# A gated linear unit: one activation and one product per tile, with only the waits that others do not imply

## The chip, the cores and the metric

The kernel runs on one core of one Trainium2 chip. The metric is the device time of a run in microseconds (us). Most runs of a kernel here agree within 0.3%. Every kernel named below was built, profiled and compared with the reference on the chip. Each was timed in rounds beside the kernel before on the same chip.

## The reference

```python
x = np.random.randn(8192, 8192).astype(np.float32)

def reference(x):
    a, b = np.split(x, 2, axis=-1)
    return a * (1 / (1 + np.exp(-b)))
```

268.4 MB go in and 134.2 MB come out, and each output element needs one sigmoid and one product.

## The kernel before

A tile is 256 rows of x, two rows (R = 2) on each of 128 partitions: 8 MB in and 4 MB out, 32 tiles. There are two slots for inputs and two for outputs. Loads are issued by the sync engine (queue 1), stores by the scalar engine (queue 10).

```python
    pool = ctx.enter_context(tc.tile_pool(name="io", bufs=2))
    for i in range(n_tiles):
        x_sb = pool.tile([P, R * n_cols], fp32)
        o_sb = pool.tile([P, R * half], fp32)
        load = nc.sync.dma_start(out=x_sb, in_=x_t[i])
        n = 4 if i == n_tiles - 1 else 1      # the last tile in 8 pieces
        w = half // n
        for r in range(R):
            for c in range(n):
                # ... a, b: columns of x_sb; cols: columns of o_sb
                nc.scalar.activation(out=b, in_=b, func=SIG)
                nc.vector.tensor_mul(out=o_sb[:, cols], in0=a, in1=b)
                if n > 1:
                    nc.scalar.dma_start(out=out_t[i, :, cols], in_=o_sb[:, cols])
        if n == 1:
            nc.scalar.dma_start(out=out_t[i], in_=o_sb)
```

The framework that builds the kernel works out the waits, and it also chooses the order of the instructions on each engine. Cut here: the lines that move the first load ahead of the program's start, which the change leaves alone.

Of the kernel before, what the change touches and what calls it, by code (L numbers as in the profile page):

```python
# [1 line left out]

# [4 lines left out]


def _tiles(ctx, tc, x, out):
    nc = tc.nc  # L10
    P = nc.NUM_PARTITIONS
    fp32 = mybir.dt.float32
    SIG = mybir.ActivationFunctionType.Sigmoid

    n_rows, n_cols = x.shape
    half = n_cols // 2
    R = 2
    n_tiles = n_rows // (P * R)
    x_t = x.rearrange("(n p r) m -> n p (r m)", p=P, r=R)
    out_t = out.rearrange("(n p r) m -> n p (r m)", p=P, r=R)  # L20

    pool = ctx.enter_context(tc.tile_pool(name="io", bufs=2))
    first = None

    for i in range(n_tiles):
        x_sb = pool.tile([P, R * n_cols], fp32)
        o_sb = pool.tile([P, R * half], fp32)
        load = nc.sync.dma_start(out=x_sb, in_=x_t[i])
        first = first or load
        n = 4 if i == n_tiles - 1 else 1  # L30
        w = half // n
        for r in range(R):
            for c in range(n):
                lo = r * n_cols + c * w
                a = x_sb[:, lo : lo + w]
                b = x_sb[:, lo + half : lo + half + w]
                cols = slice(r * half + c * w, r * half + (c + 1) * w)
                nc.scalar.activation(out=b, in_=b, func=SIG)  # L38
                nc.vector.tensor_mul(out=o_sb[:, cols], in0=a, in1=b)  # L39
                if n > 1:  # L40
                    nc.scalar.dma_start(out=out_t[i, :, cols], in_=o_sb[:, cols])  # L41
        if n == 1:
            nc.scalar.dma_start(out=out_t[i], in_=o_sb)
    return first


@with_exitstack
def kernel(
    ctx: ExitStack,
    tc: tile.TileContext,  # L50
    x: bass.AP,
    out: bass.AP,
):



    nc = tc.nc
    with ExitStack() as pools:
        _tiles(pools, tc, x, out)
    tc.close()  # L60
    tc.compile()  # L61
    blocks = nc.main_func.blocks
    entry, body = blocks[0].instructions, blocks[1].instructions
    SP = mybir.EngineType.SP
    at = next(k for k, i in enumerate(body) if i.engine == SP)
    load = body[at]
    assert load.opcode == "DMACopy" and not load.sync_info.on_wait
    del body[at]
    where = next(k for k, i in enumerate(entry) if i.engine == SP and i.opcode == "Drain")
    entry.insert(where, load)  # L70


# [1 line left out]
_INS = ['x']  # L74
_OUTS = [((8192, 4096), 'float32')]


# [23 lines left out]
```

## Time and profile before

| | before |
|---|---|
| time, median (lowest to highest) | 936.02 us (935.64 to 936.99, 6 runs) |
| span of the profiled run | 933.9 us |
| rate of all transfers | 431 GB/s |
| busy: vector engine, scalar engine | 280.9 us (30%), 230.0 us (25%) |
| load, issue to landing (median) | 45.5 us |
| store, issue to landing (median) | 41.7 us |

How to read it: the two engines that compute are idle for over two thirds of the time. "Issue to landing" runs from the moment an engine hands a transfer to its queue until the data have arrived. The prediction shows the lines of the profile that stand behind these numbers, and reads them.

### The profile page before, as it was taken

The numbers are of one execution on the slowest core, as the hardware profiler recorded it, in microseconds if no ns is written. First come the engines' busy times: TensorE is split into PE (matmuls) and PEld (weight loads), VectorE is DVE, ScalarE is ACT, GpSimd is POOL, SyncE is SP. The second block draws the span as 40 slices with busy tenths as digits, with TensorE's granted clock in tenths as the row PEclk, the third lists the DMA queues.
The fourth block names the chain that finished last, engine by engine and source line by source line (L and its number), as shares of the span: only waits on it lengthen the run. The fifth ranks groups of instructions, "written<-read, shape, count | busy, mean of one in ns | idle before, by whom it ended". The sixth has DMA issues, their size and how long they took to land.

```text
span 933.9 us, 410 instructions
## 1 busy us (share of the span) xinstructions
DVE 280.9 (30%) x70; ACT 230.0 (25%) x71; POOL 0.2 (0%) x4
## 2 busy tenths in 40 slices
DVE  0333321333213333133331333312333123331234
ACT  1313331133311333203332033320233202333023
POOL 0000000000000000000000000000000000000000
DMA  9999999999999999999999999999999999999998
GB/s 404 420 434 431 453 418 429 439 434 449 420 456 404 452 424 427 449 425 451 412 459 410 438 438 425 451 421 452 413 449 421 431 445 443 429 420 453 410 446 362
DMA packets 10226, 402.67 MB, mean 431 GB/s; under 512 B 1136, under 2 KB 1136, under 8 KB 2160
## 3 DMA queue, kind: packets, MB, share of 16 engines
q1 hardware_dynamic: 4608, 268.44, 66.5%
q10 hardware_dynamic: 5616, 134.22, 33.3%
q14 instruction: 2, 0.02, 0.0%
HBM read 268.44 MB, written 134.22 MB: 431 GB/s over the span
## 4 chain that ended last, share of the span: by engine, by line
DMA 78%; DVE 15%; ACT 6%; issue 0%; DVEq 0%; ACTq 0%
DMA x_sb<-in_x_dram 78%; DVE o_sb L39 15%; ACT x_sb L38 6%; DVEq L61 0%; ACTq L41 0%; ACTq L38 0%
## 5 line engine op out<-in xcount | busy, mean ns | idle before, releaser
L39 DVE TENSOR_TENSOR o_sb<-x_sb 128x4096 f32<-128x4096 f32 (+1 forms) x70 | 280.9, 4056 | 647.2 <-ACT x_sb L38 647.2
L38 ACT ACTIVATE x_sb<-x_sb 128x4096 f32<-128x4096 f32 (+1 forms) x70 | 228.7, 3315 | 695.9 <-DMA x_sb<-in_x_dram 691.8
L38 ACT ACT_TABLE_LOAD x1 | 1.3, 1283 | 0.8 <-PEq L85 0.8
L85 POOL MEMSET const-uint8-127<- 128x1 uint8 x1 | 0.1, 103 | 0.0
L85 POOL MEMSET const-bfloat16-1.0<- 128x1 bf16 x1 | 0.1, 102 | 0.0
L85 POOL MEMSET const-float32-0.0<- 128x1 f32 x1 | 0.1, 99 | 0.2 <-issue 0.2
L85 POOL MEMSET const-float32-1.0<- 128x1 f32 x1 | 0.1, 99 | 0.0
## 6 DMA issues: line engine op xcount, KB each, us to landing
out_dram<-o_sb ACTq DMA_DIRECT2D x31, 4096.0 KB, 41.7
out_dram<-o_sb ACTq DMA_DIRECT2D x8, 512.0 KB, 6.2
x_sb<-in_x_dram SPq DMA_DIRECT2D x32, 45.5
```

The source lines that it names most:

```text
L38: nc.scalar.activation(out=b, in_=b, func=SIG)
L39: nc.vector.tensor_mul(out=o_sb[:, cols], in0=a, in1=b)
L85: nc = _bacc.Bacc("TRN2", target_bir_lowering=False, num_devices=1)
```

## The change

Its intent: fewer and larger instructions in tiles 1 to 30 (a sigmoid of 8192 elements per partition instead of two of 4096, the product likewise), and no waits that follow from other waits. A wait for an output slot moves from the product to the sigmoid in odd tiles. Each sigmoid is pinned to the program's order on its engine. In the last tile the store of a piece follows the next piece's sigmoid.

```diff
-    pool = ctx.enter_context(tc.tile_pool(name="io", bufs=2))
+    pool = ctx.enter_context(tc.tile_pool(name="io", bufs=1))
+    xs = [pool.tile([P, R * n_cols], fp32, name=f"x_sb{k}") for k in range(SLOTS)]
+    os = [pool.tile([P, R * half], fp32, name=f"o_sb{k}") for k in range(SLOTS)]
+    def implied(later, *earlier):
+        for e in earlier:
+            tc.declare_no_dep(later.ins, e.ins, reason="follows from the waits that are kept")
...
+        load = nc.sync.dma_start(out=xs[i % SLOTS], in_=x_t[i])
+        implied(load, *old["loads"], *old["sigs"])
+        if i == 0:
+            parts = [(slice(r, r + 1), slice(0, half)) for r in range(R)]
+        elif i < n_tiles - 1:
+            parts = [(slice(0, R), slice(0, half))]
+        else:
+            # ... eight pieces of 1024 columns, as before
...
+        for k, (r, c) in enumerate(parts):
+            b = rows[:, r, 1, c]
+            sig = nc.scalar.activation(out=b, in_=b, func=SIG)
+            mul = nc.vector.tensor_mul(out=packed[:, r, c], in0=rows[:, r, 0, c], in1=b)
+            implied(sig, *old["sigs"], *old["muls"], *old["loads"])
+            implied(mul, *old["muls"], *old["loads"], *now["loads"])
+            by_sigmoid = i % 2 == 1 and len(parts) == 1
+            implied(mul, *(s for s in old["stores"] if by_sigmoid or s not in freed))
+            if by_sigmoid:
+                for s in freed:
+                    tc.add_manual_dep(sig.ins, s.ins.name, DEP, reason="frees the output slot")
+            tc.keep_in_program_order(sig)
...
+            if i == n_tiles - 1 and k > 0:
+                store(chunks[k - 1])
+        store(chunks[-1] if i == n_tiles - 1 else slice(0, R * half))
```

More of the change, by code (lines that the diff above doesn't have):

```diff
@@ L11, in _tiles @@
     P = nc.NUM_PARTITIONS
+    DEP = mybir.DependencyInfo(mybir.DependencyClass.Sync, mybir.DependencyReason.DATA)
     fp32 = mybir.dt.float32
@@ L17, in _tiles @@
     R = 2
+    SLOTS = 2
     n_tiles = n_rows // (P * R)
@@ L20, in _tiles @@
     out_t = out.rearrange("(n p r) m -> n p (r m)", p=P, r=R)
-    pool = ctx.enter_context(tc.tile_pool(name="io", bufs=2))
-    first = None
-    for i in range(n_tiles):
-        x_sb = pool.tile([P, R * n_cols], fp32)
-        o_sb = pool.tile([P, R * half], fp32)
-        load = nc.sync.dma_start(out=x_sb, in_=x_t[i])
-        first = first or load
-        n = 4 if i == n_tiles - 1 else 1
-        w = half // n
-        for r in range(R):
-            for c in range(n):
-                lo = r * n_cols + c * w
-                a = x_sb[:, lo : lo + w]
-                b = x_sb[:, lo + half : lo + half + w]
-                cols = slice(r * half + c * w, r * half + (c + 1) * w)
-                nc.scalar.activation(out=b, in_=b, func=SIG)
-                nc.vector.tensor_mul(out=o_sb[:, cols], in0=a, in1=b)
-                if n > 1:
-                    nc.scalar.dma_start(out=out_t[i, :, cols], in_=o_sb[:, cols])
-        if n == 1:
-            nc.scalar.dma_start(out=out_t[i], in_=o_sb)
@@ L44, in _tiles @@
-    return first
+    pool = ctx.enter_context(tc.tile_pool(name="io", bufs=1))
[4 more added lines that the diff above has]
+            tc.declare_no_dep(later.ins, e.ins, reason="follows from the waits that are kept")
+    gone = [{k: [] for k in ("loads", "sigs", "muls", "stores")} for _ in range(SLOTS)]
+    last_stores = [[] for _ in range(SLOTS)]
@@ new lines, in _tiles, with store @@
+    for i in range(n_tiles):
+        old = gone[i % SLOTS]
+        freed = last_stores[i % SLOTS]
+        now = {k: [] for k in old}
+        rows = xs[i % SLOTS].rearrange("p (r h m) -> p r h m", r=R, h=2)
+        packed = os[i % SLOTS].rearrange("p (r m) -> p r m", r=R)
+        load = nc.sync.dma_start(out=xs[i % SLOTS], in_=x_t[i])
+        implied(load, *old["loads"], *old["sigs"])
+        now["loads"].append(load)
+        if i == 0:
[3 more added lines that the diff above has]
+        else:
+            w = half // 4
+            parts = [
+                (slice(r, r + 1), slice(c * w, (c + 1) * w)) for r in range(R) for c in range(4)
+            ]
+        def store(cols):
+            ins = nc.scalar.dma_start(out=out_t[i, :, cols], in_=os[i % SLOTS][:, cols])
+            now["stores"].append(ins)
+        chunks = []
+        for k, (r, c) in enumerate(parts):
[10 more added lines that the diff above has]
+            tc.keep_in_program_order(sig)
+            now["sigs"].append(sig)
+            now["muls"].append(mul)
+            chunks.append(slice(r.start * half + c.start, r.start * half + c.stop))
+            if i == n_tiles - 1 and k > 0:
+                store(chunks[k - 1])
+        store(chunks[-1] if i == n_tiles - 1 else slice(0, R * half))
+        for s in now["stores"]:
+            implied(s, *old["loads"], *old["sigs"], *old["muls"], *now["loads"], *now["sigs"])
+        for k in old:
+            old[k] += now[k]
+        last_stores[i % SLOTS] = now["stores"]
```

## The prediction

> **What bounds the kernel now.** I began with the page: the row of DMA busy tenths, the row of GB/s and the table of DMA queues.
>
> ```profile
> DMA  9999999999999999999999999999999999999998
> q1 hardware_dynamic: 4608, 268.44, 66.5%
> q10 hardware_dynamic: 5616, 134.22, 33.3%
> HBM read 268.44 MB, written 134.22 MB: 431 GB/s over the span
> ```
>
> The transfer engines are busy in every slice, and the loads (queue 1) and the stores (queue 10) together fill 66.5 + 33.3 = 99.8% of the time of all 16. The vector engine is at 30% and the scalar engine at 25%. To see whether that 99.8% is a real limit I went to the transfer records of the trace. A load packet is one partition's row of 64 KB and takes 2.418 us, a store packet of 32 KB takes 1.213 us, and a 4 KB one of the last tile 0.159 us, all with almost no spread. Each of the 16 engines has 32 x 8 load packets, 31 x 8 store packets and 8 x 8 small ones: 256 x 2.418 + 248 x 1.213 + 64 x 0.159 = 619.0 + 300.8 + 10.2 = 930.0 us. The span is 933.9 us, so all that is not transfer is 3.9 us, the start before the first packet and the receipt of the last. Counting the packets that are open at each moment gives 16 (within 0.1) from the second 10 us to about 923, and 16.4 with the small packets after that.
>
> Then the chain of work that ended last, which seems to say something else:
>
> ```profile
> DMA 78%; DVE 15%; ACT 6%; issue 0%; DVEq 0%; ACTq 0%
> ...
> 101.72 3.62 ACT x_sb L38
> 105.35 0.02 issue
> 105.37 8.77 DVE o_sb L39 x2
> 114.14 0.02 issue
> 114.16 45.56 DMA x_sb<-in_x_dram
> ```
>
> The chain goes through computation for 21% of the span: a sigmoid, two products, then the load of two tiles later into the slot that these freed. It is tempting to read the 12.4 us from 101.72 to 114.14 as time that costs. But the 45.56 us of that load are not 45.56 us of transfer. Its 8 packets per engine need about 8 x (2.418 + 1.213) = 29.0 us when they alternate with stores, so for some 16.5 us it stands in the queue behind the load before it. The chain is a loop with a queue in it, and the queue takes up any change of the other terms. The views of issues and of the DMA queue's own waits say the same:
>
> ```profile
> out_dram<-o_sb ACTq DMA_DIRECT2D x31, 4096.0 KB, 41.7
> x_sb<-in_x_dram SPq DMA_DIRECT2D x32, 45.5
> ...
> SPq L28 <- DMA x_sb<-in_x_dram: 482.8, 30, 20.8
> SPq L28 <- DVE o_sb L39: 374.3, 30, 12.8
> ```
>
> Tiles follow each other every 29.05 us (loads land at 43.66, 72.9, 101.7), while a load is under way for 45.5 us and a store for 41.7. So 16.5 us before one load lands the next is already queued, and a store is issued 41.7 - 29.05 = 12.7 us before the one ahead of it has landed. The issuing queue first waits for the previous load of that slot, then for the product that frees it; the first of these waits is contained in the second.
>
> Instructions by shape give the price of computation:
>
> ```profile
> L39 DVE TENSOR_TENSOR o_sb<-x_sb 128x4096 f32<-128x4096 f32 x62 | 271.6, 4422 | 626.6 <-ACT x_sb L38 626.6
> L38 ACT ACTIVATE x_sb<-x_sb 128x4096 f32<-128x4096 f32 x62 | 220.8, 3608 | 670.1 <-DMA x_sb<-in_x_dram 670.1
> L39 DVE TENSOR_TENSOR o_sb<-x_sb 128x1024 f32<-128x1024 f32 x8 | 9.4, 1221 | 20.6 <-ACT x_sb L38 20.6
> L38 ACT ACTIVATE x_sb<-x_sb 128x1024 f32<-128x1024 f32 x8 | 7.9, 1046 | 25.9 <-DMA x_sb<-in_x_dram 21.8 <-DVE o_sb L39 4.1
> ```
>
> Both engines sleep some 20 us of each 29 us. Last, the tail after the final load:
>
> ```profile
> 919.70 2.95 ACT L38 ACTIVATE x_sb<-x_sb 128x1024 f32<-128x1024 f32 x3 [2.05 <-DVE o_sb L39]
> 927.04 1.47 ACTq L41 DMA_DIRECT2D out_dram<-o_sb  x2
> ...
> 914.63:923.00 8.37, 5.71 (x5) 5.90 (x6) 0.00 (x0) 1.00 0.93 399
> 923.00:931.50 8.50, 3.64 (x4) 2.00 (x2) 0.00 (x0) 1.00 1.01 412
> ```
>
> In the second pair the columns before the last two are engine times; the last two are DMA share and GB/s. Even here, with small sigmoids, products and stores one behind the other, the transfer engines are full to about 931.4: most of the store of tile 30 is still queued at 914.63 (it lands at 923.0), and the eight last pieces follow it.
>
> **What the Trainium skill says.** "DMA: Bandwidth & Descriptors", Specifications, gives a fabric ceiling of 435 GB/s for 16 engines; the trace has 431 over the span and 437 and 430 in two single-tile stretches (43.66 to 72.9, 72.9 to 101.7), so the kernel stands at it. The same page, "Queues, rings and completion order", says that each engine takes turns between the queues that have work, a packet at a time. Loads and stores of a tile are 8 packets each per engine here, and 66.5% against 33.3% is what one for one of 64 and 32 KB gives, so the trace agrees. "ScalarE: Activation LUTs", What ACT_TABLE_LOAD costs, gives 186 ns + 0.833 ns per element for an activation without pointer operands; the median here is 3.601 us for 4096 and 1.040 for 1024, a slope of 2.561 / 3072 = 0.834 ns and a constant of 0.19 us. "Perfetto Trace Analysis", Optimizing Scalar/DVE Operations, says that grouping operations helps throughput "if the engine is saturated"[...].
>
> **The change part by part.**
> (1) Tiles 1 to 30 get one sigmoid and one product of 8192 elements. The sigmoid costs 0.19 + 8192 x 0.834 ns = 7.02 us. The product's slope is (4.420 - 1.218) / 3072 = 1.042 ns, its constant 0.15 us, so 8.69 us. Instructions go from 70 to 2 + 30 + 8 = 40 on each engine. Busy time falls a little: per tile from a union of 7.12 to 7.02 us and from 8.76 to 8.69, so by about 30 x 0.1 = 3 us and 30 x 0.07 = 2 us in total. None of it lies on a limit.
> (2) The product now starts after the whole sigmoid and not after half of it. From sigmoid start to the freed slot and the store it takes 7.02 + 8.69 + 0.07 = 15.8 us instead of 12.4, so 3.4 us later in each of 30 tiles. Were this on the path, with two slots, it would be 3.4 / 2 per tile, 30 x 1.7 = 51 us. It is not: the next load is issued 16.5 - 3.4 = 13.1 us before the load ahead of it lands, and a store 12.7 - 3.4 = 9.3 us before the store ahead of it does. Receipt and start-up of a transfer take some 2 us of these (the last 512 KB pieces take 4.8 us for about 1.3 us of packets). Neither queue runs dry, so the order of packets doesn't change. Cost: 0.
> (3) Waits removed: a sequencer step of 0.02 to 0.06 us in front of each sigmoid and load, hidden. The wait of the load for the previous load disappears as a name; its time goes to the wait for the product. Cost: 0.
> (4) On odd tiles the sigmoid takes the wait for the store of two tiles before, which was the product's. That store lands at 56.12 + 41.8 = 97.9 where the load it competes with lands at 101.64, so it has 3.7 us to spare. As the packet order stays, both landing times stay although the store is issued later. Cost: 0.
> (5) In the last tile each store is issued one sigmoid later in the program, and the order is fixed. Before, sigmoids went in bunches of 3, 3 and 2 and the product waited some 1.5 us twice. Now a piece costs the scalar engine 1.05 + 0.36 + 0.05 = 1.46 us, and the last store should go out near 927.1 instead of 928.2. The transfer engines are full until 931.4, so of that 1.1 us I count 0 to 0.3.
> The first tile keeps its two parts and the first load stays hoisted. Sum: 0 to -0.3 us, so 936.13 goes to about 935.9.
>
> **Rivals.** First, the longer loop shows, as the chain of waits suggests, up to 51 us: 987 us. For it speaks only the chain; against it the full transfer engines and 13.1 us of queue. Second, the new sigmoid wait on odd tiles eats its 3.7 us of spare, because stores issued 3.4 us later also land 3.4 us later. Then 0.3 us would still be left; a further slip of 1 us per odd tile would delay the slot by 1 us only, again into the queue. That makes 936 as well, perhaps 937 if the drift adds up. Third, the tail was issue-bound after all, and the full 1.1 us is gained: 935.0. Fourth, the pattern of reads and writes at the memory shifts by 3.4 us and changes the rate of transfer: packets of fixed duration speak against it; 0.3% of it would be 3 us either way.
>
> **Range and chances.** The three runs before lie between 935.86 and 936.99, and the transfer total fixes 930.0 of the 933.9 us in the profile. I predict 935.9 us, and 934.8 to 937.2 for 8 times in 10. Faster by over 2% would need fewer bytes or a higher rate than the ceiling: 0.01. Slower needs both queues dry: 0.015. Within 2%: 0.975.
>
> **What would show it.** DMA busy 9 in all slices and near 431 GB/s. Load issue to landing 45.5 - 3.4 = 42.1 us and store 41.7 - 3.4 = 38.3: the queue giving back what the computation took. The chain of waits with ACT near 12% (7.0 of 58.1 us), DVE 15% and DMA 72%. Sigmoids of 8192 near 7.02 us and products near 8.69, still 20 us idle before them for ACT. The queue's own waits on the product alone, near 860 us over 30. I am wrong if landing times stay at 45.5 while tiles come over 30 us apart, if sigmoids of odd tiles are released by a store and tile spacing grows, or if DMA slices fall under 9.

## The result and the profile after

The changed kernel takes 935.76 us (median of 6 runs, 934.76 to 936.71), the kernel before 936.02 us. The ratio is 0.9996, with a 95% interval of 0.9983 to 1.0009: the same. A ratio here is the mean time of one kernel's fast runs over that of the other's of the same rounds, so it is not quite the ratio of the medians. Executions over 1.5% slower than the fastest of the same kernel are left out of the means. The outputs are right.

First the page of the changed kernel: DMA busy tenths, queues, the chain that ended last, and the issues.

```profile
DMA  9999999999999999999999999999999999999998
q1 hardware_dynamic: 4608, 268.44, 66.5%
q10 hardware_dynamic: 5616, 134.22, 33.3%
HBM read 268.44 MB, written 134.22 MB: 431 GB/s over the span
...
DMA 73%; DVE 15%; ACT 12%; issue 0%; ACTq 0%
...
out_dram<-o_sb ACTq DMA_DIRECT2D x31, 4096.0 KB, 36.0
x_sb<-in_x_dram SPq DMA_DIRECT2D x32, 42.2
```

The first four lines are those of before, to the digit. The chain moved: ACT went from 6% to 12% and DMA from 78% to 73%, at an unchanged time. Load issue to landing fell from 45.5 to 42.2 us. In the chain in order of time (start, duration, what), one turn looks like this:

```profile
104.19 7.04 ACT x_sb L71
111.25 8.70 DVE o_sb L72
119.97 42.14 DMA x_sb<-in_x_dram
```

Landing to next issue is 119.97 - 104.19 = 15.8 us, before it was 12.4. The load that follows takes 42.1 us instead of 45.6. A turn is 58.0 us (104.19 to 162.19), and was 58.1 (101.72 to 159.80). So the 3.4 us that the computation took came out of the time that the load stands in its queue.

The groups by shape, then the DMA queue's own waits:

```profile
L72 DVE TENSOR_TENSOR o_sb<-x_sb 128x8192 f32<-128x8192 f32 x30 | 260.8, 8692 | 608.4 <-ACT x_sb L71 608.4
L71 ACT ACTIVATE x_sb<-x_sb 128x8192 f32<-128x8192 f32 x30 | 210.9, 7029 | 654.8 <-DMA x_sb<-in_x_dram 654.8
...
SPq L51 <- DVE o_sb L72: 861.8, 30, 33.3
```

The scalar engine still sleeps 654.8 / 30 = 21.8 us before each sigmoid, always for a load. No wait of the sigmoids for a store appears. The issuing queue has one kind of wait for a slot in place of two, and its 861.8 us are nearly the 482.8 + 374.3 = 857.1 us of before under one name: removing a wait that another one contains removed a line of the profile here and no time.

### The profile page after: what moved, and what is told of

The parts are those of the page before. It is cut to its first block, busy times and chain, and to the rows that moved or that the text cites. A ratio compares the mean times of both kernels' runs of the same rounds, so it can differ in the third digit from the quotient of the medians.

```text
span 934.9 us, 271 instructions
## 1 busy us (share of the span) xinstructions
DVE 279.0 (30%) x40; ACT 227.6 (24%) x41; POOL 0.2 (0%) x4
## 3 DMA queue, kind: packets, MB, share of 16 engines
q1 hardware_dynamic: 4608, 268.44, 66.5%
q10 hardware_dynamic: 5616, 134.22, 33.3%
## 4 chain that ended last, share of the span: by engine, by line
DMA 73%; DVE 15%; ACT 12%; issue 0%; ACTq 0%
DMA x_sb<-in_x_dram 73%; DVE o_sb L72 15%; ACT x_sb L71 12%; ACTq L65 0%; ACTq L71 0%
## 5 line engine op out<-in xcount | busy, mean ns | idle before, releaser
L72 DVE TENSOR_TENSOR o_sb<-x_sb 128x8192 f32<-128x8192 f32 (+2 forms) x40 | 279.0, 6985 | 649.5 <-ACT x_sb L71 649.5
L71 ACT ACTIVATE x_sb<-x_sb 128x8192 f32<-128x8192 f32 (+2 forms) x40 | 226.3, 5663 | 698.8 <-DMA x_sb<-in_x_dram 696.7
## 6 DMA issues: line engine op xcount, KB each, us to landing
x_sb<-in_x_dram SPq DMA_DIRECT2D x32, 42.2
```

The source lines that it names most:

```text
L71: sig = nc.scalar.activation(out=b, in_=b, func=SIG)
L72: mul = nc.vector.tensor_mul(out=packed[:, r, c], in0=rows[:, r, 0, c], in1=b)
```

## The experiments

Three theories stood at the start. Queue: transfers are the bound, and waiting loads and stores absorb a longer computation. Loop: the computation lies on the path, as the chain suggests. Cancelling: grouping costs something, and another part of the change gives it back. A fourth, order, came from the first results.

### Grouping alone: group_alone

```diff
+        if 0 < i < n_tiles - 1:
+            rows = x_sb.rearrange("p (r h m) -> p r h m", r=R, h=2)
+            packed = o_sb.rearrange("p (r m) -> p r m", r=R)
+            b = rows[:, :, 1, :]
+            nc.scalar.activation(out=b, in_=b, func=SIG)
+            nc.vector.tensor_mul(out=packed, in0=rows[:, :, 0, :], in1=b)
+            nc.scalar.dma_start(out=out_t[i], in_=o_sb)
+            continue
```

> The grouping of tiles 1 to 30 alone, on the kernel before, with its waits and its tail. Queue theory (the transfer queues absorb a longer computation): 936 us, ratio 0.998 to 1.002; load issue to landing near 42.1 us and the computation 15.8 us between landing and next issue. Loop theory (the computation lies on the path that the chain of waits shows): 30 x 1.7 us more, so some 987 us, ratio 1.05. Cancelling theory (grouping costs a little and the reordered tail and fewer waits give as much back): 937 to 938 us, ratio 1.001 to 1.002 or more.

Measured: 945.18 us (942.62 to 951.28, 6 runs), ratio 1.0106 (1.0083 to 1.0130). The queue theory missed here by 9 us, and the loop theory, at 51 us, by more. Its timeline around tiles 4 and 5 (start, duration, engine, what):

```profile
132.32 7.03 ACT L35 ACTIVATE x_sb<-x_sb 128x8192 f32<-128x8192 f32 x1 [21.97 <-DMA x_sb<-in_x_dram]
139.38 8.69 DVE L36 TENSOR_TENSOR o_sb<-x_sb 128x8192 f32<-128x8192 f32 x1 [20.31 <-ACT x_sb L35]
158.89 7.03 ACT L35 ACTIVATE x_sb<-x_sb 128x8192 f32<-128x8192 f32 x1 [19.55 <-DMA x_sb<-in_x_dram]
158.92 16.12 ACTq L37 DMA_DIRECT2D out_dram<-o_sb  x2
```

The product of tile 4 is done at 148.07, but its store goes out at 158.92, right after the sigmoid of tile 5 has started. The scalar engine works its stream in order. In the built program that sigmoid stands ahead of this store, and a sigmoid that waits for its load holds up everything behind it. The built stream has this in 7 pairs of tiles:

```
sigmoid 4, sigmoid 5, store 4, store 5, sigmoid 6, store 6, sigmoid 7, store 7, sigmoid 8, sigmoid 9, store 8, store 9, ...
```

In the kernel before, the built order is the program's in all tiles but the last, whose small pieces go in bunches. So grouping, with nothing else said, made the framework choose another order. This is what the next runs test.

The transfer records (the start, duration and size of each packet in the trace) show where the 9 us went in this run: from 923 to 943 us, after the last load, a transfer engine was idle for some 7 us in the mean over the 16, and the load packets took 3.6 us more per engine than in the changed kernel (624.8 against 621.2 us).

### The change without the grouping: waits_alone

```diff
-        if i == 0:
+        if i < n_tiles - 1:
             parts = [(slice(r, r + 1), slice(0, half)) for r in range(R)]
-        elif i < n_tiles - 1:
-            parts = [(slice(0, R), slice(0, half))]
...
-            by_sigmoid = i % 2 == 1 and len(parts) == 1
+            by_sigmoid = i % 2 == 1 and i < n_tiles - 1 and k == 0
```

> The change without the grouping: a sigmoid and a product for each row as before, but its declared waits, the slot wait on the sigmoid of odd tiles and its order of stores in the last tile. Queue theory: 936 us, ratio 0.998 to 1.001, landing times of 45 us or, if the order of packets at the start falls as in the changed kernel, 45 for loads and 39 for stores. Cancelling theory: 934 to 935 us, ratio under 0.999. Loop theory: unchanged, as the computation of a tile stays 12.4 us.

Measured: 936.18 us (935.10 to 936.42, 5 runs), ratio 1.0000 (0.9988 to 1.0012). Fewer waits and the new order of the last tile give nothing back. The cancelling theory, in the form in which these parts gain time, falls.

### The kernel before, again: before_again

The edit is none.

> The kernel before itself, as a control: ratio 0.999 to 1.001, which gives the noise against which the other two are read. Second question, from the changed kernel's trace, where loads landed 2.4 us later against the stores from tile 1 on and stores 36.0 us after issue and not 38.3: is that one packet of difference at the start, which comes by chance? If so, this trace may show load 1 landing at either 43.7 or 46.1 us; if it belongs to the change, it lands at 43.7 again. All theories: 936 us.

Measured: 935.90 us (935.71 to 936.60, 5 runs), ratio 0.9999 (0.9986 to 1.0012), which is the noise. Its trace has the second tile's sigmoid start at 45.59, where the first trace of the same kernel has 43.68. Its stores take 39.0 us and not 41.7. So the phase between loads and stores differs between two runs of one kernel, here by 1.9 us, which is less than a load packet (2.4 us), and the changed kernel's 46.13 is not clearly the change's.

### The grouping, pinned: group_pinned

```diff
-            nc.scalar.activation(out=b, in_=b, func=SIG)
+            sig = nc.scalar.activation(out=b, in_=b, func=SIG)
+            tc.keep_in_program_order(sig)
```

(in the grouped tiles of group_alone; nothing else)

> The run with grouping alone took 945 us. Its build put the sigmoid of the next tile ahead of the store of this tile on the scalar engine's stream in 7 pairs of tiles, so these stores were issued only after the next load had landed. This kernel is the same with one line more, which pins each grouped sigmoid behind what stands before it in the program, the store of the tile before; all waits and the tail are those of the kernel before. Order theory (the 9 us are the order's): 936 us, ratio 0.999 to 1.001, load issue to landing near 42.1. Rival (grouping with the waits of the kernel before costs 9 us, and the declared waits take it away): 943 to 947, ratio near 1.01.

Measured: 938.16 us (937.75 to 938.48, 5 runs), ratio 1.0017 (1.0005 to 1.0029). One line of order takes away 7 of the 9 us (medians, each over the kernel before of its own rounds: 9.3 and 1.9 us). For the rest, here is the end of its timeline, and under it the stretch from 910 to 914 (the last two columns are DMA share and GB/s; a packet counts in the stretch in which it starts):

```profile
893.86 8.69 DVE L37 TENSOR_TENSOR o_sb<-x_sb 128x8192 f32<-128x8192 f32 x1 [20.30 <-ACT x_sb L35]
913.34 1.06 ACT L47 ACTIVATE x_sb<-x_sb 128x1024 f32<-128x1024 f32 x1 [19.51 <-DMA x_sb<-in_x_dram]
913.45 0.34 ACTq L38 DMA_DIRECT2D out_dram<-o_sb  x1
...
910.00:914.00 4.00, 0.00 (x0) 0.66 (x1) 0.00 (x0) 1.00 0.12 49
```

The store of tile 30 was free to go at 902.55 and went at 913.45, behind unpinned sigmoids of tile 31. With no further load and no store in a queue, the transfer engines ran dry. The 12% overstates it, because load packets that had started before 910 were still running: in the transfer records 14.8 of 16 packets are open from 910 to 912 and 1.3 from 912 to 914. The idle time around it, 2.2 us in the mean over the 16 engines, is the size of what is missing.

### Pinned to the last tile: group_pinned_to_last

```diff
-            nc.scalar.dma_start(out=out_t[i], in_=o_sb)
+            stored = nc.scalar.dma_start(out=out_t[i], in_=o_sb)
...
-                nc.scalar.activation(out=b, in_=b, func=SIG)
+                sig = nc.scalar.activation(out=b, in_=b, func=SIG)
+                if i == n_tiles - 1:
+                    tc.add_manual_dep(sig.ins, stored.ins.name, ORDER, reason="behind the store before")
```

(ORDER sets the place in the stream only; it adds no wait)

> The pinned grouping took 938.2 us, and its trace shows the store of tile 30 issued 0.1 us after the last load had landed, 11 us after its product ended: the small sigmoids of the last tile, not pinned, had gone ahead of it, and the transfer engines were busy for only 12% of the four us from 910 to 914. Here these sigmoids are pinned behind that store too; waits and the rest of the tail stay those of the kernel before. Order theory: the last 2 us come back, 936 us, ratio 0.999 to 1.001. Rival (the waits of the kernel before, or its bunched tail, cost them): 938 us again, ratio 1.0015 or more.

Measured: 936.05 us (935.68 to 936.52, 5 runs), ratio 1.0001 (0.9987 to 1.0015). With the waits and the bunched last tile of the kernel before, grouping costs nothing that these runs can see (the interval is 0.3% wide) once every store keeps its place. So all of the 9 us came from the order.

### The change without its pin: change_unpinned

```diff
-            tc.keep_in_program_order(sig)
```

> The change without its one line that pins the sigmoids to the program's order; the declared waits and the slot wait on the sigmoid of odd tiles stay. The build then puts the sigmoid of each fourth tile ahead of the store before it (7 times). Order theory: slower than before, 940 to 948 us, ratio 1.005 to 1.013, with a pair of stores issued together in these places. Rival (declared waits are what keeps it at 936): 936 us, ratio under 1.002.

Measured: 945.54 us (943.71 to 947.50, 4 runs), ratio 1.0097 (1.0084 to 1.0110). The declared waits don't protect the order. This one line of the change is worth 9.8 us (945.54 - 935.76, which were timed in different rounds). Here they are not idle time, unlike most of those in group_alone:

```profile
DMA  9999999999999999999999999999999999999998
...
q1 hardware_dynamic: 4608, 268.44, 66.9%
```

66.9% of the 945.7 us span is 632.7 us of load packets per engine, against 66.5% of 934.9 = 621.7 us in the changed kernel, for the same bytes: 11 us more. In the transfer records a load packet still takes 2.418 us in the median, but 331 of the 4096 take over 2.5 us, against 35 in the changed kernel. From 400 us on most of them come in groups of 14 to 31 (there are 16 engines). What lengthens them was not settled.

### A longer computation: product_one_and_half, product_twice, product_three

These do the product of tiles 1 to 30 again, over half the columns, all of them, or all of them twice, with the same result:

```diff
+            if 0 < i < n_tiles - 1:
+                for w in (half // 2,):        # twice: (half,)   three times: (half, half)
+                    nc.vector.tensor_mul(
+                        out=packed[:, r, :w], in0=rows[:, r, 0, :w], in1=rows[:, r, 1, :w]
+                    )
```

> The change with the product of tiles 1 to 30 repeated over half its columns: 4.4 us more, 20.1 us between landing and next load. The product done twice cost 1.7% and more, which is a seventh of what the loop theory asks but more than the queue theory allowed. If a margin is used up between 15.8 and 24.5 us, this one should still be inside it: 936 us, ratio 0.999 to 1.002, load issue to landing near 37.8 us. Loop theory: 30 x 4.4 / 2 = 66 us more, 1002 us. If the cost grew evenly with the length, half of what twice cost: 942 to 950 us.

> The change with the product of tiles 1 to 30 done twice over (same result): 8.69 us more between landing and the next load and store, 24.5 us in place of 15.8. Queue theory: the queue of loads had 13.1 us in hand, so some 4 us remain. The queue of stores had 7 to 9 us in hand and may run empty for a short while, in which loads go alone; the engines stay busy: 936 to 942 us, ratio under 1.007, load issue to landing near 33.5 us. Loop theory: 30 x 8.69 / 2 = 130 us more, 1066 us.

> The product done three times: 33.1 us of computation for a tile, over the 29.05 us that its transfers take. As the sigmoid is pinned behind the store of the tile before, nothing of two tiles overlaps, and the computation itself is the bound. Queue theory: a tile takes some 33.5 us, 30 x 4.5 = 135 us more at most, 1050 to 1070 us, and DMA slices fall under 9. Loop theory: 30 x 17.4 / 2 = 261 us more, 1197 us. If it stayed under 950, the idea of the limit would be wrong altogether.

| computation, landing to next issue | time | ratio | load, issue to landing |
|---|---|---|---|
| 15.8 us (the change) | 935.76 | 0.9996 | 42.2 |
| 20.2 us (one and a half) | 936.03 (5 runs) | 1.0000 (0.9987 to 1.0013) | 37.7 |
| 24.5 us (twice) | 951.81 to 953.54 (3 fast runs) | 1.0173 (1.0158 to 1.0187) | 33.6 |
| 33.2 us (three times) | 1081.49 (4 runs) | 1.1540 (1.1523 to 1.1557) | 32.6 |

One and a half is free, as expected, and the load gave back 4.5 us. The loop theory wanted 1002 us. Twice costs 16 us where the loop theory wants 130. But it also costs more than the 6 us that I had allowed, so that expectation is a miss. Three of its six runs were slower still (981.2 to 983.3), at the same granted clock of 1.0 as the fast ones; I have no cause for them, and whether they are the machine's state or the kernel's own stays open. Its page, its waits, and two stretches of its profiled run (951.81 us):

```profile
DMA  9999999999999999999999999999999999999998
...
HBM read 268.44 MB, written 134.22 MB: 424 GB/s over the span
...
ACT x_sb L71 <- DMA x_sb<-in_x_dram: 395.1, 18, 25.0
ACT x_sb L71 <- DMA out_dram<-o_sb: 314.4, 14, 23.8
...
100.00:550.00 450.00, 267.73 (x31) 112.47 (x16) 0.00 (x0) 1.00 1.00 434
550.00:930.00 380.00, 219.02 (x26) 84.83 (x13) 0.00 (x0) 1.00 1.00 415
```

For the first 550 us it moves 434 GB/s, as the changed kernel does. Then the rate falls to 415, with a DMA share of 1.00 in both. From 563 us on the transfer records show groups of lengthened load packets (15 to 29 in most of them), as in change_unpinned. 14 sigmoids were released by a store and not by a load: the wait on odd tiles had 6 us to spare in the changed kernel, and here the store lands 0.2 us after the load. But it does so from tile 3 on, also while the rate still holds, so that wait alone is not the cost. Why the rate holds for half of the run and then gives way was not settled.

Three times was expected at 1050 to 1070 us and measured 1081, a miss by 11 us. There the idle of the scalar engine is for the product (639.4 us in 24 waits), so the computation is the bound:

```profile
DMA  9979888898889988889888998889988899888998
...
ACT x_sb L71 <- DVE o_sb L75: 639.4, 24, 26.7
```

Its transfer records show lengthened packets too. 29 times no load packet is open for more than 1.3 us, and each time the 16 load packets that follow take 1.3 to 1.5 us longer than 2.418 in the median. That time is booked as busy. In these gaps the stores have mostly run out as well (2 of 16 packets open on average), so the run doesn't show that an empty load queue alone does it. It isn't enough that no load packet is open: the kernel before has 22 such gaps in its first trace, with stores on all 16 engines, and the load packets after them keep their 2.42 us. And in the kernels before and after, the 16 load packets that begin just before the very first store (from 36 or 38 us on) take 3.5 to 3.7 us in the median, though 16 load packets were open all the time. Whether the groups in product_twice and change_unpinned have the same cause is not shown.

### Nearly no computation: sixteen_columns

Its output is wrong, which doesn't matter for the time.

```diff
+    for o in os:
+        nc.gpsimd.memset(o, 0.0)
...
+            whole = slice(r.start * half + c.start, r.start * half + c.stop)
+            c = slice(c.start, c.start + 16)
             b = rows[:, r, 1, c]
...
-            chunks.append(slice(r.start * half + c.start, r.start * half + c.stop))
+            chunks.append(whole)
```

> A wrong result on purpose: sigmoid and product work on 16 columns of each part, the output slots are filled with zeros once, all transfers and waits stay. It shows the time with next to no computation, so what any cheaper computation could still gain. Queue theory: the transfers alone are the bound, 934.5 to 936.5 us, ratio 0.998 to 1.001, load issue to landing near 57 us. Loop theory: 15 us less in the loop of two tiles, up to 30 x 7.5 us less unless the transfer rate stops it, so clearly under 930. In between (a little of the computation shows at the end): 931 to 934.

Measured: 950.72 us (950.06 to 951.11, 4 runs), ratio 1.0157 (1.0143 to 1.0172). All three expectations missed: with next to no computation it is slower. Its end, in stretches and in the timeline:

```profile
922.00:927.00 5.00, 0.00 (x0) 0.00 (x0) 0.00 (x0) 1.00 0.26 111
927.00:936.00 9.00, 0.00 (x0) 0.07 (x1) 0.00 (x0) 1.00 0.07 29
936.00:948.00 12.00, 1.33 (x8) 1.55 (x8) 0.00 (x0) 1.00 0.88 350
...
935.93 0.32 ACT L76 ACTIVATE x_sb<-x_sb 128x16 f32<-128x16 f32 x2 [29.03 <-DMA x_sb<-in_x_dram]
```

Most of the loss lies at the end, where the last load lands at 935.9 us and not at 916.8 as in the changed kernel. From 927 to 936 the transfer records show a single packet open at each moment (a share of 0.07 is one engine in 16): one engine is late and holds up the landing of the last load. This leaves the engines idle for 10 us in the mean from 922 to 934, the larger part of the 15 us. What makes it late was not settled.

A smaller part has another cause. Stores go out here 0.6 us after a load lands (51.51 to 52.06 in the second tile), so they keep up with the loads, and at the end next to none is left over. Between the last load packet and the first packet of the last tile's stores all engines are idle for 2.8 us, and these 4 MB, 10 us of packets, follow alone. In the changed kernel 54 of the 128 packets of tile 30's store have not started when the last load lands, and the transfer engines stay full from there to about 931 us.

So this run doesn't show the time without computation: the late engine covers it.

### The last tile in one piece: last_tile_whole, last_tile_whole_mended

```diff
-        elif i < n_tiles - 1:
+        else:
             parts = [(slice(0, R), slice(0, half))]
-        else:
-            # ... eight pieces
```

> The changed kernel with the last tile as one sigmoid, one product and one store as well. After the last load there is no further load in the queue, and the store of tile 30 is drained near 922. Queue theory: here the computation is seen. The last load lands near 916.7, the store goes out 15.8 us later near 932.5 and needs 9.7 us of packets and some 3 to 4 us of start and receipt, so the span ends near 946 and the time is near 948 us, ratio 1.012. If the tail were hidden too: 936. The loop theory says the same of the tail, so this run tells only whether the reading of the tail holds.

The first try was faulty: it stored only one of the last tile's two rows, so the result was wrong, with 939.87 us (5 runs) for 2 MB too few. The second stores both:

```diff
-        store(chunks[-1] if i == n_tiles - 1 else slice(0, R * half))
+        store(slice(0, R * half))
```

> The last tile as one piece, with the fault of the earlier try (it stored only half of that tile) mended. That try gave 939.9 us with 2 MB in its last store; the full 4 MB need 4.9 us more at the measured packet times. Queue theory: 944 to 946 us, ratio 1.009 to 1.011, with the transfer engines idle between the end of the store of tile 30 and the last store's start. If the last tile's computation were hidden as that of the others is: 936.

Measured: 944.56 us (943.71 to 945.60, 4 runs), correct, ratio 1.0090 (1.0074 to 1.0106), as expected. This expectation started from the time of the faulty try; the one made before it, 948 us, was 3.4 us too high.

```profile
922.00:925.00 3.00, 2.35 (x1) 0.61 (x1) 0.00 (x0) 1.00 0.00 0
925.00:933.00 8.00, 6.34 (x1) 0.00 (x0) 0.00 (x0) 1.00 0.15 66
933.00:942.00 9.00, 0.00 (x0) 0.00 (x0) 0.00 (x0) 1.00 0.95 408
```

Here nothing is queued, and the same sigmoid and product that are free in 30 tiles are seen: 11 us in which almost nothing moves, and then 4 MB. This is the queue theory from its other side.

## Why the prediction was right

The time was 935.76 us against 935.9, and the mechanism was the one named: the transfers stay the bound, and the queue of loads gives back what the computation takes. By its own steps:

- (1), the prices, held: 7.029 us for the sigmoid against 7.02, and 8.692 us for the product against 8.69. Busy time fell by 2.4 us for the sigmoids (228.7 to 226.3) and 1.9 us for the vector engine.
- (2), the longer computation, held. Landing to next issue is 15.8 us, loads take 42.2 us against 42.1, and the next load is issued 13.2 us before the one ahead lands, against 13.1. Stores take 36.0 us against 38.3; the control showed 39.0 for the kernel before, so most of this miss is the phase that comes by chance. The strongest support is from outside the change: 4.4 us more are free as well, and without a queue the computation is seen (last_tile_whole_mended).
- (3), the removed waits, held: waits_alone has ratio 1.0000, and the queue's wait for the product is 861.8 us against some 860.
- (4), the wait on odd tiles, held: no sigmoid was released by a store. Its spare was 5.8 to 6.5 us and not 3.7, since the stores happened to come earlier against the loads; before_again has 5.5 to 6.5 us. In product_twice it is used up.
- (5), the last tile: the last store follows the last load's landing by 11.7 us (916.78 to 928.46) where it was 13.5, so 1.8 us earlier and not 1.1. Nothing of it shows in the time, within the 0 to 0.3 us allowed.

Two things were incomplete, though neither moved the number. Step (2) took for granted that a store goes out as soon as its product ends; that is the work of one line, the pin to the program's order, which the prediction names only for the last tile. Without it the same grouping costs 9 us, and the same reasoning, used for group_alone, gave 936 us and missed. On this point the prediction was lucky: the kernel that it was made for has the line. No rival named the order. The fourth came nearest: it let the rate of transfer change, and set packets of fixed duration against it. They aren't fixed in change_unpinned and product_twice, where the DMA row is full in every slice and the kernels are 1% to 1.7% slower. The prediction speaks of empty queues only for a loss of over 2%, and has no term for such a smaller one. And time in hand at the queue isn't all: in product_twice the next load is still issued 4.5 us (median) before the one ahead lands, and yet between 4.4 and 8.7 us more of computation begins to cost. Where exactly, and why only in the second half of that run, was not settled.

Three of its readings don't hold as they stand. The shares of 66.5% and 33.3% follow from the packets' number and duration in any order, so they don't show that loads and stores alternate. The transfer records do: with each packet joined to the one that ended as it began, most load packets (2542 of 3601 between 60 and 880 us) start 3.6 to 3.7 us after the one before on their engine, which is 2.418 + 1.213. "Some 2 us" for start-up and receipt is too low by its own figures, 4.8 - 1.3 = 3.5 us. And "almost no spread" passes over 29 load packets of over 3 us, all in the first 41 us.

None of the kernels tried beats the two: every correct one with its stores in order, its last tile in pieces and at most 20.2 us of computation lies at 936 us.

## What to carry to other kernels

In a chain of waits, look at whether the transfer in it is longer than its own packets need: the surplus is queueing, and here it paid for 4.4 us more of computation than the change itself needs, but not in full for 8.7. After merging instructions, read the built order of an engine that both computes and issues stores: a store behind a sigmoid that waits for the next load is late by that wait (10.9 us for tile 4 of group_alone). A full DMA row says that the engines are occupied and not that they move bytes at full rate (434 and 415 GB/s at the same share of 1.00 in product_twice), so compare GB/s and the queue's share times the span. Take short stretches of that row with care, since a packet counts where it starts; the transfer records say what was open. And leave some store traffic queued for the end, where it hides the last tile's computation (last_tile_whole_mended, 8.6 us).

## What the Trainium skill lacked or had wrong

- "DMA: Bandwidth & Descriptors" gives a first-byte latency and a fixed cost of a transfer but does not say that packets themselves can lengthen: in product_three by 1.3 to 1.5 us over 2.418 us, 29 times, after moments in which loads and nearly all stores had run out, and counted as busy time. In product_twice the rate fell from 434 to 415 GB/s at a DMA share of 1.00.
- The same page's Specifications list about 358 GB/s as the limit of HBM for a core beside the fabric's 435. A core here moved 431 GB/s, loads and stores together. The row derives its figure from a stack's rate over two cores; only further sections say that it holds with both cores at work.
- "Perfetto Trace Analysis", Optimizing Scalar/DVE Operations, tells when grouping or splitting helps but not that either may change the order in which the build places other instructions of the same engine. In group_alone that cost 9 us, and holding the program's order took it back (group_pinned, group_pinned_to_last). No page that I read has it.
- No page that I read has the phase between two queues that comes by chance: loads 1.7 to 1.9 us later, and stores of 39.0 or 41.7 us, in two traces of one kernel whose spans (934.5 and 933.9 us) differ by less than 0.1%.
